# Two encoder layers on one core: memory keys at the head of layer 1, first loads reordered, more transposes by DMA

## The chip, the cores and the metric

One Trainium2 chip, one of its cores. The time is the device time of one execution in microseconds (us). The kernel before took 2009.22 us (median of three runs, 2007.9 to 2009.52). The core's engines each run their own program in order: PE (TensorE, the matmuls and the transposes through the identity), ACT (ScalarE), DVE (VectorE), POOL (GpSimd) and SP (SyncE, which here only issues loads). DMA queues belong to SP, ACT and POOL.

## The reference

A trunk of two layers (the depth is set to 2) over 256 tokens of width 2048, in float32, with 256 memory tokens:

```python
for l in range(DEPTH):                       # 2
    h = rms_norm(x, g_mix[l])
    if l % 2 == 0:                           # layer 0: spatial gating
        z = h @ w_in_a[0]                    # 2048 x 3584: u | v (1536 each), q_mem (512)
        tok_out = chunked_spatial_gating(...)   # u * (w_s @ rms_norm(v) + b_s), after a gelu
    else:                                    # layer 1: grouped-query attention, 12 heads on 4
        z = h @ w_in_b[0]                    # 2048 x 3072: q (1536), k, v (512 each), q_mem (512)
        tok_out = gqa_axial_attention(...)   # per-head rms norm, rotary, softmax
    mem_out = memory_attention(q_mem, mem, g_mem[l], w_mem_kv[l], g_mq[l], g_mk[l])
    x = x + concatenate([tok_out, mem_out]) @ w_out[l]
    x = x + swiglu(rms_norm(x, g_ffn[l]), w_gate_up[l], w_down[l])
```

`memory_attention` normalises the memory, multiplies it with `w_mem_kv` (keys: its first 512 columns, values: the next 512), normalises queries and keys per head, and does a softmax attention over 256 memory tokens with four heads.

## The kernel before, in words

**Products.** Each float32 operand is split into a high and a low part; `matmul3` (L181 to L183) issues high x high, low x high and high x low. `transpose4` (L185) turns four 128x128 blocks on PE (L187). `Linear` (L269) computes 256 tokens x 512 columns over K = 2048, that is 16 chunks of 128, in 96 matmuls of 128x512. Weights come as units of four K chunks: one load on SP's queue (L279), casts to the high part on ACT in pieces of two chunks (L265) and the low part on DVE (L266). Four raw tiles and three high and low tiles go round, so a cast waits until PE is done with the unit three before.

**Activations.** The residual stream lies in SBUF as `X[t][j]`: token tile t (0, 1) by a quarter j of the width (512 columns). For a linear its pieces are needed transposed and multiplied with the norm's gain, as high part (ACT, L225 or L237) and low part (DVE, L226 or L238). The norm's 1/rms itself is applied behind the product, so a linear may start ahead of it. A piece is turned either on PE (`norm_piece`, L209) or by `turned` (L189): ACT copies the words' halves apart (L194), issues a DMA transpose on its queue (L195), and later copies the halves back (L200), for which it waits until the transfer has landed. `add_residual` (L608) does that for one j, plus the squares of the norm (`square_sum`, L207, two per piece). In the feed-forward's last part of layer 0, `residual_turns` (L624) does it for layer 1's input: j=0,1 after the first pair of output columns, j=2,3 at the very end.

**Memory.** `prep` (L574) loads eight tiles of the transposed memory on POOL's queue (L577) and multiplies each with its gain three ticks later (`gained_pair`, L231: two products on ACT at L237 and two on DVE at L238 per tile). `keys` and `values` are one linear each over these tiles. In both layers they stand behind the memory queries' linear; in layer 1 that is behind all other linears of the mixer but the output's.

**The order.** `later(n, fn)` puts work n ticks ahead on a queue; a linear ticks twice in four K chunks. This sets the order in which instructions are recorded. A scheduler with its own model of times then lays down each engine's program; the engines run these strictly in order.

**The first linear.** In layer 0 it takes `x_t`, the transposed input, in eight loads, between them the weights in units of one, one and two chunks, and the eight loads of X (L135). Its outputs go through a Gelu (L727), whose scale is the norm, so all sixteen squares of X come before it. Meanwhile nine small matmuls warm PE up (L686).

**The feed-forward** (L776 on) uses a Strassen-like scheme in pairs of column blocks; no line of it is touched except `residual_turns`.

Of the kernel before, what the change touches and what calls it, by code (L numbers as in the profile page):

```python
# [17 lines left out]
P = 128  # L18
# [10 lines left out]
NB = 512  # L29
# [26 lines left out]
def encoder(ctx: ExitStack, tc: tile.TileContext, x, x_t, mem, mem_t, columns, w_in_a, g_v_a, spatial_t, w_in_b,  # L56
# [212 lines left out]
    class Linear:  # L269
# [3 lines left out]
            self.parts, self.w, self.n0, self.left, self.first, self.raw = parts, w, n0, nk, True, {}  # L273
            self.acc = [psa.tile([P, NB], F32, tag="acc", name=nm("acc")) for _ in range(NT)]

        def fetch(self, k0, n):
            raw = wp.tile([P, KC4, NB], F32, tag="raw", name=nm("raw"), bufs=RAW_TILES)
            src = self.w[k0 * P:(k0 + n) * P, self.n0:self.n0 + NB]
            nc.sync.dma_start(raw[:, :n], src.rearrange("(c p) n -> p c n", p=P))  # L279
            self.raw[k0] = raw  # L280

        def run(self, units):
            for k0, n in units:
                if k0 not in self.raw:
                    self.fetch(k0, n)
                raw = self.raw.pop(k0)
                parts = halves(raw[:, :n], n, KC2)
                for s in range(0, n, KC2):
                    m = min(KC2, n - s)
                    self.left -= m  # L290
                    for t in range(NT):
                        for c in range(m):
                            matmul3(self.acc[t], self.parts.get(k0 + s + c, t), parts[s + c],
                                    self.first and c == 0, self.left == 0 and c == m - 1)
                    self.first = False
                    tick()
            return self.acc
# [188 lines left out]
                nc.vector.tensor_tensor(lo[pr][:, :, ts], src, hi[pr][:, :, ts].bitcast(F32), ALU.subtract)  # L486
        return hi, lo

    def attend(qn, waits, keys, values, kv_of, kc0, parts):


        st = {}

        def head(p, h):
            return p[0][h // 2][:, h % 2, :], p[1][h // 2][:, h % 2, :]

        def queries():
            st["qT"] = heads_T(qn)

        def scores(pr):  # L500
            for h in (2 * pr, 2 * pr + 1):
# [13 lines left out]
                rcp = small(2)  # L515
                nc.vector.reciprocal(rcp, sm)
                for t in range(NT):
                    nc.vector.tensor_scalar(pe[:, t * S:(t + 1) * S], pe[:, t * S:(t + 1) * S], rcp[:, t:t + 1], None,
                                            ALU.mult)
                st["p", h] = pe  # L520

        def turn(pr):
            for h in (2 * pr, 2 * pr + 1):
                pn = st["p", h]
                pt = misc()
                for t in range(NT):
                    for kc in range(2):
                        nc.tensor.transpose(pt[:, kc * S + t * P:kc * S + (t + 1) * P],  # L528
                                            pn[:, t * S + kc * P:t * S + (kc + 1) * P], ident)
                st["t", h] = split(pt, [P, NB])  # L530

        def weigh(pr):
            V = values()
            po = misc()
            for hh in range(2):
                h = 2 * pr + hh
                kv = kv_of(h)
                phi, plo = st["t", h]
# [29 lines left out]
    class Memory:  # L568
# [5 lines left out]
        def prep(self, delay, apart):  # L574
            def load(i):
                m = big(shape=[P, 2, S])
                nc.gpsimd.dma_start(m, mem_t[:, 2 * i:2 * i + 2])  # L577
                later(3, lambda: gained_pair(m, i, gslice("mem", self.l), self.parts, big))
                if self.l == 0:
                    j, t = i // 2, i % 2  # L580
                    rows = big()
                    nc.gpsimd.dma_start(rows, mem[0, t * P:(t + 1) * P, j * NB:(j + 1) * NB])
                    later(3, lambda: squares(rows, j, t))

            def squares(rows, j, t):
                self.norm.add(rows, t, j)
                if (j, t) == (3, NT - 1):
                    self.norm.finish(self.r)

            for i in range(8):  # L590
                later(delay + apart * i, lambda i=i: load(i))

        def keys(self):
            acc = linear(self.parts, w_mem_kv[self.l], 0)
# [6 lines left out]
        def values(self):  # L601
            self.V = scaled(linear(self.parts, w_mem_kv[self.l], NB), self.r)

        def attend(self, acc, r, parts):
            attend(head_norm(acc, r, ghead[f"mq{self.l}"]), (4, 13, 17, 19), lambda: self.kT, lambda: self.V, lambda h: h,
                   TOK // P, parts)

    def add_residual(acc, j, norm, g, parts, dma):  # L608

# [12 lines left out]
            later(1 + t, lambda t=t: turn(t))  # L622

    def residual_turns(j, norm, g, parts):  # L624
        add_residual(None, j, norm, g, parts, j < 2)


    hT = Parts()
# [1 line left out]
    for l in range(DEPTH):  # L630
# [4 lines left out]
        if l == 0:  # L635
# [27 lines left out]
                nc.vector.tensor_tensor(v4(sb[t][c]), v4(sps), bcast4(bcol[:, 4 * c:4 * c + 4]), ALU.add)  # L663

            def turn_u(us, t, c):
                tp = misc()
                transpose4(us, tp)
                hi, lo = split(v4(tp), [P, 4, P])
                for i in range(4):
                    cat.put(4 * c + i, t, hi[:, i, :], lo[:, i, :])  # L670

            def load_turned(i, engine=nc.sync):
                turned_x[i] = big(shape=[P, 2, S])
# [13 lines left out]

            turned_x = {}
            lin = Linear(hT, w, TOK)
            load_turned(0, nc.scalar)  # L690
            nc.scalar.dma_start(cols, columns)
            nc.scalar.activation(junk[:, :8], mhalf, AF.Square)
            warm_up(9)
            lin.fetch(0, 1)
            lin.fetch(1, 1)
            load_turned(1)
            lin.fetch(2, 2)
            first_piece(0)
            lin.run([(0, 1)])
            load_turned(2)  # L700
            load_turned(3)
            lin.run([(1, 1)])
            first_piece(1)
            lin.run([(2, 2)])
            for i in range(2, 8):
                first_piece(i)
                if i % 2 == 0 and i < 6:
                    load_turned(i + 2)
                    load_turned(i + 3)
                lin.run([(2 * i, KC2)])  # L710
            for t in range(NT):
                for j in range(4):
                    load_x(t, j)
            load_tables(0)
            for j in range(4):
                first_squares(j)
            norm.finish()
            acc = lin.acc
            m.prep(1, 2)
            for i in range(3):  # L720
                later(10 + i, lambda i=i: load_spatial(i))
            for c in range(3):
                if c:
                    acc = linear(hT, w, TOK + c * NB)
                for t in range(NT):
                    v[t][c] = big()
                    nc.scalar.activation(v[t][c], acc[t], AF.Gelu, scale=norm.r[t])  # L727
                    square_sum(v[t][c], ssv[t][:, 2 * c:2 * c + 2])
            for t in range(NT):
                gate_rms(t)  # L730
                for c in range(3):
                    later(3 + 3 * t + c, lambda t=t, c=c: gate(t, c))
            m.attend(linear(hT, w, 2 * TOK), norm.r, cat)
            m.keys()
            m.values()
            for c in range(3):
# [6 lines left out]
        else:  # L743
            w = w_in_b[0]
            own = {}
            load_tables(1)
            m.prep(20, 2)
            acc = linear(hT, w, TOK)
            kn = head_norm(acc, norm.r, ghead["k"], True)

# [5 lines left out]
            for c in range(3):  # L756
                acc = linear(hT, w, c * NB)
                attend(head_norm(acc, norm.r, ghead["q"], True), (5, 6, 10, 13), lambda: own["k"], lambda: own["v"],
                       lambda h, c=c: (4 * c + h) // 3, 4 * c, cat)
            m.attend(linear(hT, w, TOK + 2 * MEMW), norm.r, cat)  # L760
            m.keys()
            m.values()

        hF = Parts()
# [130 lines left out]
```

## Time and profile before

| What | Value |
|---|---|
| time, median of 3 runs | 2009.22 us |
| the profiled execution's time | 2011.89 us |
| its span, first to last instruction | 2010.0 us |
| busy: PE, DVE, ACT, POOL | 1994.3, 1587.4, 1204.0, 60.3 us |
| mean granted PE clock | 0.998 |
| moved by DMA | 413.85 MB, 206 GB/s on average |
| first matmul of layer 1 | at 1007.5 us |

A row of the groups reads: line, engine, operation, written tile <- read tiles, shape, count, then busy us and mean ns of one, then the engine's idle time before them and what ended it. A row of the chain reads: start, length, what. Times are us from the span's start. In the names, `raw` is a loaded weight tile, `whi`/`wlo` its two parts, `h` and `a` activations, `m` a small PSUM tile, `acc` an accumulator, `x` the residual stream, `cols` the gains, `junk` the unused output of a square.

### The profile page before, as it was taken

The page shows a single profiled execution, that of the slowest core. Times are in us where ns is not written, and L with a number is a line of the kernel's source. Part 1 is how long each engine was busy: PE and PEld are TensorE (multiplying, and loading weights), DVE is VectorE, ACT ScalarE, POOL GpSimd, SP SyncE. Part 2 cuts the span into 40 slices and gives each one's busy share as a digit, 9 for nine tenths or more (in the row PEclk, how much of TensorE's full clock was granted, in tenths as well). Part 3 has the DMA queues.
Part 4 walks back from the last instruction along what each step waited for, and adds up shares of the span by engine and source line. Part 5 has one row for each costly group of instructions (what it writes and reads, how often), then busy time and mean ns, then how long its engine had stood idle before and what let it go on. Part 6 is the DMA issues. An engine that isn't in the chain of part 4 may idle for free.

```text
span 2010.0 us, 23977 instructions
## 1 busy us (share of the span) xinstructions
PE 1994.3 (99%) x8996; PEld 1652.5 (82%) x8996; DVE 1587.4 (79%) x1686; ACT 1204.0 (60%) x1450; POOL 60.3 (3%) x88
## 2 busy tenths in 40 slices
PE   8999999999999999999999999999999999999999
PEld 7888888888888888887888888888888888888787
DVE  5755558998988989886666876699988889888877
ACT  7755475666446664465765665856764467644662
POOL 2100001000000000000011000010000000000000
PEclk9999999999999999999999999999999999999999
DMA  9854675676666776657766434756766567665674
GB/s 354 288 177 159 194 214 182 206 218 212 220 209 189 213 217 223 208 187 230 224 220 199 163 122 154 217 188 198 229 214 219 189 199 232 214 214 188 199 209 147
DMA packets 266404, 413.85 MB, mean 206 GB/s; under 512 B 74640, under 2 KB 74896, under 8 KB 266288
## 3 DMA queue, kind: packets, MB, share of 16 engines
q1 hardware_dynamic: 199808, 387.62, 58.1%
q10 hardware_dynamic: 63792, 16.19, 4.7%
q0 software_dynamic: 2688, 8.52, 1.3%
q8 instruction: 70, 1.15, 0.2%
q14 instruction: 46, 0.38, 0.1%
HBM read 394.45 MB, written 2.10 MB: 197 GB/s over the span
## 4 chain that ended last, share of the span: by engine, by line
PE 93%; DMA 3%; DVE 2%; ACT 1%; issue 1%; ACTq 0%; SPq 0%; DVEq 0%
PE acc L183 27%; PE acc L182 27%; PE acc L181 27%; PE m L183 4%; PE m L181 4%; PE m L182 4%; DMA a<-a 2%; DVE wlo L266 1%; ACT whi L265 1%; PE m L187 1%; DMA a<-in_x_t 0%; DMA x<-in_x 0%; PE m L528 0%; PE m L661 0%; DMA raw<-in_w_in_a 0%
## 5 line engine op out<-in xcount | busy, mean ns | idle before, releaser
L266 DVE TENSOR_TENSOR wlo<-raw,whi 128x2048 fp32r<-128x2048 f32 (+2 forms) x465 | 841.2, 1824 | 280.4 <-ACT whi L265 267.7
L265 ACT CAST whi<-raw 128x2048 fp32r<-128x2048 f32 (+2 forms) x465 | 705.9, 1538 | 474.8 <-PE acc L182 375.1
L181 PE MATMUL acc<-whi,h 128*128 128x512 f32 x1440 | 561.9, 391 | 4.5 <-ACT whi L265 2.7
L182 PE MATMUL acc<-whi,h 128*128 128x512 f32 x1440 | 561.6, 390 | 0.0
L183 PE MATMUL acc<-wlo,h 128*128 128x512 f32 x1440 | 516.3, 391 | 0.8 <-DVE wlo L266 0.8
L181 PE MATMUL acc<-whi,a 128*128 128x512 f32 x1062 | 414.3, 391 | 1.2 <-DVE a L459 1.2
L182 PE MATMUL acc<-whi,a 128*128 128x512 f32 x1062 | 414.4, 390 | 0.0
L183 PE MATMUL acc<-wlo,a 128*128 128x512 f32 x1062 | 399.1, 390 | 0.2 <-DVE wlo L266 0.2
L181 PEld LDWEIGHTS acc<-whi,h 128*128 128x128 f32 x1440 | 270.6, 188 | 61.1 <-ACT whi L265 4.0
L183 PEld LDWEIGHTS acc<-wlo,h 128*128 128x128 f32 x1440 | 270.8, 188 | 58.6 <-DVE wlo L266 2.9
L182 PEld LDWEIGHTS acc<-whi,h 128*128 128x128 f32 x1440 | 270.9, 188 | 56.2 <-DVE h L238 0.4
L181 PEld LDWEIGHTS acc<-whi,a 128*128 128x128 f32 x1062 | 199.8, 188 | 43.2 <-DVE a L459 1.6
L183 PEld LDWEIGHTS acc<-wlo,a 128*128 128x128 f32 x1062 | 199.8, 188 | 41.7 <-DVE wlo L266 0.6
L182 PEld LDWEIGHTS acc<-whi,a 128*128 128x128 f32 x1062 | 199.7, 188 | 40.9
L265 ACT CAST whi<-T 128x1536 fp32r<-128x1536 f32 x82 | 121.4, 1480 | 103.4 <-PE acc L182 93.8
L266 DVE TENSOR_TENSOR wlo<-T,whi 128x1536 fp32r<-128x1536 f32 x82 | 143.6, 1751 | 11.0 <-ACT whi L265 11.0
L364 DVE TENSOR_TENSOR T<-raw 128x1024 f32<-128x1024 f32 x82 | 100.0, 1220 | 21.5 <-DMA raw<-in_w_gate_up 20.7
L181 PE MATMUL m<-whi,a 128*128 128x512 f32 x264 | 102.8, 390 | 0.2 <-ACT whi L265 0.2
L183 PE MATMUL m<-wlo,a 128*128 128x512 f32 x264 | 102.8, 389 | 0.1
L182 PE MATMUL m<-whi,a 128*128 128x512 f32 x264 | 102.7, 389 | 0.0
L200 ACT COPY sg<-a 128x1024 uint16<-128x1024 uint16 x44 | 51.5, 1169 | 47.0 <-DMA a<-a 46.8
L441 DVE TENSOR_TENSOR e<-acc,e 128x512 f32<-128x512 f32 x88 | 58.1, 684 | 2.5 <-PE acc L183 2.5
(120 smaller groups left out, 1432.9 us busy)
## 6 DMA issues: line engine op xcount, KB each, us to landing
raw<-in_w_gate_up SPq DMA_DIRECT2D x352, 512.0 KB, 4.4
raw<-in_w_down SPq DMA_DIRECT2D x176, 512.0 KB, 4.9
raw<-in_w_out SPq DMA_DIRECT2D x32, 1024.0 KB, 5.3
raw<-in_w_in_a SPq DMA_DIRECT2D x24, 1024.0 KB, 5.3
raw<-in_w_in_b SPq DMA_DIRECT2D x24, 1024.0 KB, 5.2
raw<-in_w_mem_kv SPq DMA_DIRECT2D x16, 1024.0 KB, 5.1
a<-in_mem_t POOLq DMA_DIRECT2D x16, 256.0 KB, 5.3
raw<-in_w_in_a SPq DMA_DIRECT2D x7, 512.0 KB, 7.2
```

The source lines that it names most:

```text
L181: nc.tensor.matmul(out, lhsT=a[0], rhs=b[0], start=start, stop=False)
L182: nc.tensor.matmul(out, lhsT=a[1], rhs=b[0], start=False, stop=False)
L183: nc.tensor.matmul(out, lhsT=a[0], rhs=b[1], start=False, stop=stop)
L187: nc.tensor.transpose(dst[:, c * P:(c + 1) * P], src[:, c * P:(c + 1) * P], ident)
L200: nc.scalar.copy(halves, back.rearrange("p (h n) -> p n h", h=2))
L265: nc.scalar.copy(hi[:, cut], raw[:, cut])
L266: nc.vector.tensor_tensor(lo[:, cut], raw[:, cut], hi[:, cut].bitcast(F32), ALU.subtract)
L364: nc.vector.tensor_tensor(T[:, :2], raw[:, 1:4:2], w01, ALU.add)
L441: nc.vector.tensor_tensor(o[t][n], self.bank[name], o[t][n], op)
```

## The change

Four things, which the diff below shows:

1. *The start.* The gains (`cols`) are loaded first on ACT's queue and all `x_t` on SP's. The first linear's weights come in units of four chunks, cut into loads of 256 or 512 KB; X is loaded behind all of them. The squares, the norm's end and the first Gelu are put off by ticks (1 to 4, 5 and 6). The warm-up has sixteen matmuls. The memory's loads are called with `prep(3, 2)`.
2. *Layer 0's turns.* The six tiles of u and the memory attention's four probability tiles are turned by `turned` and no longer on PE (24 and 16 transposes), the latter with other waits (4, 13, 17, 21).
3. *Between the layers.* The residual pieces j=2,3 are turned by DMA too (16 transposes of PE fewer).
4. *Layer 1.* `prep(-4, 1)` and the memory keys' linear stand ahead of the layer's other linears; `prep(0, 1)` loads and multiplies the memory again for the values, whose linear is last, behind the memory queries and their attention (waits 4, 5, 9, 11).

`prep` now counts its ticks from one point, and work whose tick has passed is recorded at once (`soon`).

```diff
@@ class Linear
-        def fetch(self, k0, n):
-            raw = wp.tile([P, KC4, NB], F32, tag="raw", name=nm("raw"), bufs=RAW_TILES)
-            src = self.w[k0 * P:(k0 + n) * P, self.n0:self.n0 + NB]
-            nc.sync.dma_start(raw[:, :n], src.rearrange("(c p) n -> p c n", p=P))
-            self.raw[k0] = raw
+        def fetch(self, k0, n, cuts=None):
+            if k0 not in self.raw:
+                self.raw[k0] = wp.tile([P, KC4, NB], F32, tag="raw", name=nm("raw"), bufs=RAW_TILES)
+            for c, m in cuts or [(0, n)]:
+                src = self.w[(k0 + c) * P:(k0 + c + m) * P, self.n0:self.n0 + NB]
+                nc.sync.dma_start(self.raw[k0][:, c:c + m], src.rearrange("(c p) n -> p c n", p=P))
@@ def attend(..., dma=False), def turn(pr)
+                if dma:
+                    def halves_of(whole, h=h):
+                        hi, lo = split(whole.rearrange("p (t k) n -> p k t n", t=NT), [P, 2, NT, P])
+                        st["t", h] = [a.rearrange("p k t n -> p (k t n)") for a in (hi, lo)]
+
+                    turned(pn, 2, halves_of, True)
+                    continue
@@ class Memory, def prep(self, delay, apart)
-                later(3, lambda: gained_pair(m, i, gslice("mem", self.l), self.parts, big))
+                soon(delay + apart * i + 3, lambda: gained_pair(m, i, gslice("mem", self.l), self.parts, big))
...
+            now = clock[0]
+
+            def soon(at, fn):
+                if now + at <= clock[0]:
+                    fn()
+                else:
+                    later(now + at - clock[0], fn)
+
             for i in range(8):
-                later(delay + apart * i, lambda i=i: load(i))
+                soon(delay + apart * i, lambda i=i: load(i))
@@ def residual_turns(j, norm, g, parts)
-        add_residual(None, j, norm, g, parts, j < 2)
+        add_residual(None, j, norm, g, parts, True)
@@ layer 0, def turn_u(us, t, c)
-                tp = misc()
-                transpose4(us, tp)
-                hi, lo = split(v4(tp), [P, 4, P])
-                for i in range(4):
-                    cat.put(4 * c + i, t, hi[:, i, :], lo[:, i, :])
+                def parts(whole):
+                    hi, lo = split(whole, [P, 4, P])
+                    for i in range(4):
+                        cat.put(4 * c + i, t, hi[:, i, :], lo[:, i, :])
+
+                turned(us, 2, parts, True)
@@ layer 0, the start (after)
+            nc.scalar.dma_start(cols, columns)
+            load_turned(0)
+            lin.fetch(0, KC4, [(0, 1), (1, 1)])
+            warm_up(16)
...
+            lin.run([(0, KC4)], 1)
...
+            lin.run([(8, KC4)])
             for t in range(NT):
                 for j in range(4):
                     load_x(t, j)
             load_tables(0)
+            for i in (6, 7):
+                first_piece(i)
+            lin.run([(12, KC4)])
             for j in range(4):
-                first_squares(j)
-            norm.finish()
+                later(1 + j, lambda j=j: first_squares(j))
+            later(5, norm.finish)
             acc = lin.acc
-            m.prep(1, 2)
+            m.prep(3, 2)
...
+            later(6, lambda: gated(0, acc))
+            for c in (1, 2):
+                gated(c, linear(hT, w, TOK + c * NB))
...
-            m.attend(linear(hT, w, 2 * TOK), norm.r, cat)
+            m.attend(linear(hT, w, 2 * TOK), norm.r, cat, (4, 13, 17, 21), True)
@@ layer 1
-            m.prep(20, 2)
+            m.prep(-4, 1)
+            m.keys()
             acc = linear(hT, w, TOK)
             kn = head_norm(acc, norm.r, ghead["k"], True)
...
-            m.attend(linear(hT, w, TOK + 2 * MEMW), norm.r, cat)
-            m.keys()
+            m.prep(0, 1)
+            m.attend(linear(hT, w, TOK + 2 * MEMW), norm.r, cat, (4, 5, 9, 11), False)
             m.values()
```

How the engines' programs change at the places the prediction speaks of. ACT at the start, where the first linear ends (`x_0`, `x_1` are X; L727 and, in the changed kernel, L750 are the Gelu; each cast is of weights). Before:

```order
L265 CAST whi_315<-raw_313 128x1024 [waits DMAHW1_49,DVE_49,PE_49]
L207 ACTIVATE junk,s_1_91<-x_1_85 128x256 [waits DMAHW3_49,Activation_49]
L207 ACTIVATE junk,s_1_91<-x_1_85 128x256 [waits Activation_49]
L207 ACTIVATE junk,s_2_92<-x_1_87 128x256 [waits DMAHW7_49,Activation_49]
L207 ACTIVATE junk,s_2_92<-x_1_87 128x256 [waits Activation_49]
L265 CAST whi_383<-raw_381 128x1024 [waits DMAHW2_49,DVE_49,PE_49]
L265 CAST whi_383<-raw_381 128x1024
L727 ACT_TABLE_LOAD [waits PE_49]
L727 ACTIVATE a_371<-acc_103,s_64_363 128x512 [waits Pool_49]
```

and now, from the last cast of the first linear's weights to the first cast of the second's (between the rows with `x_0` and `x_1` stand eleven more squares):

```order
L265 CAST whi_307<-raw_238 128x1024 [waits DMAHW1_49]
L207 ACTIVATE junk,s_1_91<-x_0_84 128x256 [waits DMAHW2_49]
L207 ACTIVATE junk,s_1_91<-x_0_84 128x256 [waits Activation_49]
L207 ACTIVATE junk,s_2_92<-x_0_86 128x256 [waits DMAHW6_49,Activation_49]
...
L207 ACTIVATE junk,s_2_92<-x_1_87 128x256 [waits DMAHW1_49,Activation_49]
L207 ACTIVATE junk,s_2_92<-x_1_87 128x256 [waits Activation_49]
L750 ACT_TABLE_LOAD [waits PE_49]
L750 ACTIVATE a_471<-acc_103,s_62_447 128x512 [waits Pool_49]
L265 CAST whi_341<-raw_339 128x1024 [waits DMAHW2_49,DVE_49]
```

Before, three of the first linear's casts stood between the squares, and the second linear's first cast (`whi_383`) stood ahead of the table load. Now all sixteen squares stand in one run, and that cast (`whi_341`) stands behind the Gelu.

ACT between the layers, from the squares of the last residual pieces on. Before (`m` are PE's transposes, `whi_7745` and `whi_7777` weights of layer 1's first linear):

```order
L265 CAST whi_7745<-raw_7743 128x1024
L207 ACTIVATE junk,s_415_2564<-x_1_87 128x256 [waits DVE_49,Activation_49]
L225 ACTIVATE h_7624<-m_7619,cols 128x128 [waits PE_49]
...
L207 ACTIVATE junk,s_415_2564<-x_1_87 128x256 [waits Activation_49]
L225 ACTIVATE h_7624<-m_7619,cols 128x128 [waits DVE_49]
L225 ACTIVATE h_7641<-m_7636,cols 128x128 [waits PE_49]
...
L265 CAST whi_7777<-raw_7775 128x1024 [waits DMAHW5_49,PE_49]
```

and now (each L237 row is the first of a memory tile's two products: `a_7593` is K chunks 0 and 1 of the keys' linear, `a_7601` 2 and 3, `a_7647` 4 and 5, `a_7691` 6 and 7; the fourth copy back and four more tiles follow):

```order
L207 ACTIVATE junk,s_410_2558<-x_1_87 128x256 [waits Activation_49]
L237 ACTIVATE a_7593<-a_7591,cols 128x256 [waits DMASW6_49]
L237 ACTIVATE a_7601<-a_7599,cols 128x256 [waits DMASW7_49]
...
L194 COPY a_7635<-x_1_85 128x1024
L195 DMA_TRANSPOSE a_7636<-a_7635 128x8x128 [waits Activation_49]
L194 COPY a_7641<-x_1_85 128x1024
L200 COPY a_7635<-a_7636 128x1024 [waits DMAHW3_49]
L195 DMA_TRANSPOSE a_7642<-a_7641 128x8x128 [waits Activation_49]
L237 ACTIVATE a_7647<-a_7607,cols 128x256 [waits DMASW0_49]
...
L200 COPY a_7667<-a_7668 128x1024 [waits DMAHW5_49]
L195 DMA_TRANSPOSE a_7674<-a_7673 128x8x128 [waits Activation_49]
L237 ACTIVATE a_7691<-a_7609,cols 128x256 [waits DMASW1_49]
```

Before, no product at L237 stood near the boundary; the memory came later. Now all eight tiles' products stand behind the last squares, six of them between or behind the four turns. On PE the keys' 96 matmuls are the first of layer 1, and none of another linear stands between them.

POOL between the layers, now (`in_mem_t` is the memory, L165 and L168 are the norm's scale and pow):

```order
L585 DMA a_7591<-in_mem_t 128x512 [waits DMAHW5_49,DMASW6_49]
L165 TENSOR_SCALAR s_1241_7681<-s_1240_7679 128x1 [waits DVE_49]
L165 TENSOR_SCALAR s_1244_7687<-s_1243_7685 128x1 [waits DVE_49]
L160 TENSOR_SCALAR a_7584<-a_7584 128x128 [waits DMASW2_49]
L168 TENSOR_TENSOR s_1242_7683<-s_1241_7681,mhalf 128x1 [waits Pool_49]
L168 TENSOR_TENSOR s_1245_7689<-s_1244_7687,mhalf 128x1 [waits Pool_49]
L160 TENSOR_SCALAR a_7584<-a_7584 128x128 [waits DMASW4_49]
L585 DMA a_7599<-in_mem_t 128x512 [waits DMASW7_49]
```

One memory tile is loaded ahead of the norm's end, the others behind it; before, all eight stood further down. At the start POOL now issues four memory loads right behind the first two gains, ahead of the norm; before, the first memory load stood behind it.

More of the change, by code (lines that the diff above doesn't have):

```diff
@@ L274, in __init__, with run @@
             self.acc = [psa.tile([P, NB], F32, tag="acc", name=nm("acc")) for _ in range(NT)]
[L276 to L282 removed]
+        def fetch(self, k0, n, cuts=None):
[4 more added lines that the diff above has]
+                nc.sync.dma_start(self.raw[k0][:, c:c + m], src.rearrange("(c p) n -> p c n", p=P))
+        def run(self, units, step=KC2):
             for k0, n in units:
@@ L286, in run @@
                 raw = self.raw.pop(k0)
-                parts = halves(raw[:, :n], n, KC2)
+                parts = halves(raw[:, :n], n, step)
                 for s in range(0, n, KC2):
@@ L487, in heads_T, with attend @@
         return hi, lo
-    def attend(qn, waits, keys, values, kv_of, kc0, parts):
+    def attend(qn, waits, keys, values, kv_of, kc0, parts, dma=False):
         st = {}
@@ L582, in load @@
                     nc.gpsimd.dma_start(rows, mem[0, t * P:(t + 1) * P, j * NB:(j + 1) * NB])
-                    later(3, lambda: squares(rows, j, t))
+                    soon(delay + apart * i + 3, lambda: squares(rows, j, t))
             def squares(rows, j, t):
@@ L602, in values, with attend @@
             self.V = scaled(linear(self.parts, w_mem_kv[self.l], NB), self.r)
-        def attend(self, acc, r, parts):
-            attend(head_norm(acc, r, ghead[f"mq{self.l}"]), (4, 13, 17, 19), lambda: self.kT, lambda: self.V, lambda h: h,
-                   TOK // P, parts)
+        def attend(self, acc, r, parts, waits, dma):
+            attend(head_norm(acc, r, ghead[f"mq{self.l}"]), waits, lambda: self.kT, lambda: self.V, lambda h: h, TOK // P,
+                   parts, dma)
     def add_residual(acc, j, norm, g, parts, dma):
@@ L689, in encoder @@
             lin = Linear(hT, w, TOK)
-            load_turned(0, nc.scalar)
             nc.scalar.dma_start(cols, columns)
+            load_turned(0)
+            lin.fetch(0, KC4, [(0, 1), (1, 1)])
             nc.scalar.activation(junk[:, :8], mhalf, AF.Square)
-            warm_up(9)
-            lin.fetch(0, 1)
-            lin.fetch(1, 1)
+            warm_up(16)
             load_turned(1)
-            lin.fetch(2, 2)
+            lin.fetch(0, KC4, [(2, 2)])
+            for i in (2, 3):
+                load_turned(i)
             first_piece(0)
[L699 to L702, printed above, removed]
+            lin.fetch(4, KC4, [(0, 2), (2, 2)])
             first_piece(1)
-            lin.run([(2, 2)])
-            for i in range(2, 8):
-                first_piece(i)
[L707 to L710, printed above, removed]
+            for i in (4, 5):
+                load_turned(i)
+            lin.run([(0, KC4)], 1)
+            lin.fetch(8, KC4, [(0, 2), (2, 2)])
+            for i in (6, 7):
+                load_turned(i)
+            for i in (2, 3):
+                first_piece(i)
+            lin.run([(4, KC4)])
+            lin.fetch(12, KC4, [(0, 2), (2, 2)])
+            for i in (4, 5):
+                first_piece(i)
+            lin.run([(8, KC4)])
             for t in range(NT):
@@ L714, in encoder, with gated @@
             load_tables(0)
+            for i in (6, 7):
+                first_piece(i)
+            lin.run([(12, KC4)])
             for j in range(4):
-                first_squares(j)
-            norm.finish()
+                later(1 + j, lambda j=j: first_squares(j))
+            later(5, norm.finish)
             acc = lin.acc
-            m.prep(1, 2)
+            m.prep(3, 2)
             for i in range(3):
                 later(10 + i, lambda i=i: load_spatial(i))
-            for c in range(3):
-                if c:
-                    acc = linear(hT, w, TOK + c * NB)
+            def gated(c, acc):
                 for t in range(NT):
```

## The prediction

> **What bounds the kernel now.** I read the page first (busy shares, the chain that ended last), then the chain row by row at the places the change touches, then the windows around them.
>
> ```profile
> span 2010.0 us, 23977 instructions
> PE 1994.3 (99%) x8996; PEld 1652.5 (82%) x8996; DVE 1587.4 (79%) x1686; ACT 1204.0 (60%) x1450; POOL 60.3 (3%) x88
> PE 93%; DMA 3%; DVE 2%; ACT 1%; issue 1%; ACTq 0%; SPq 0%; DVEq 0%
> ```
>
> The chain is TensorE for 93%. So a change can gain only by giving PE less to do, or by closing the few places where it stands idle; and it can lose wherever PE's next operand comes late. What PE does per instruction, and that it does not pause between layer 0 and layer 1, the chain shows there (start, length, what):
>
> ```profile
> 1007.42 0.23 PE acc L183
> 1007.65 0.23 PE acc L181
> ...
> 1014.04 0.87 PE m L187 x8
> ```
>
> A 128x512 matmul takes 0.227 us of PE's time (a linear's 96 are 21.8 us), eight transposes take 0.87 us. Layer 1's first matmul follows layer 0's last at 1007.5 with no gap. Windows of the stretches concerned (window, length, busy of PE, PEld, DVE, ACT, POOL, granted clock, DMA share, GB/s):
>
> ```profile
> 0.00:34.00 34.00, 28.76 (x115) 22.50 (x116) 17.72 (x29) 26.39 (x62) 4.92 (x17) 0.95 0.98 342
> 1007.50:1030.00 22.50, 22.50 (x109) 18.71 (x108) 15.08 (x27) 14.88 (x34) 3.10 (x6) 1.00 0.58 191
> 1153.00:1163.00 10.00, 8.02 (x34) 6.20 (x33) 8.88 (x25) 7.46 (x26) 2.52 (x2) 0.83 0.46 161
> 1187.00:1192.00 5.00, 3.73 (x25) 3.06 (x24) 3.81 (x13) 5.00 (x17) 0.00 (x0) 1.00 0.00 1
> ```
>
> The boundary costs nothing today. The start is bound by the loads (DMA share 0.98). In layer 1's attention PE idles 1.98 + 1.27 us, and the clock of 0.83 over 10 us means some 3.4 us at half speed, 1.7 us lost: 5.0 us in all.
>
> **Transposes taken from PE.** u: 6 tiles of 4 = 24; layer 0's memory probabilities 16; residual pieces j=2,3 16. 56 x 0.87/8 = **-6.1 us**, if what they become is covered. A DMA turn is a copy at L194, an issue at L195 and a copy back at L200, all on ScalarE, which runs in order and stands at L200 until the transfer lands.
>
> ```profile
> L195 ACTq DMA_TRANSPOSE a<-a x4: 1248/1248/1249, 972.8 to 986.2; - x4
> DMA to landing us min/median/max: 3.0/4.0/5.2
> ...
> L195 ACTq DMA_TRANSPOSE a<-a x4: 1248/1249/1299, 364.6 to 408.3; - x4
> DMA to landing us min/median/max: 3.9/5.8/9.2
> ```
>
> These are L195's four turns shortly before the boundary and four amid layer 0's feed-forward: issue 1.25 us, landing 3.0 to 5.2 and up to 9.2. ScalarE's waits (total, times, longest):
>
> ```profile
> ACT whi L265 <- PE acc L182: 468.9, 183, 4.6
> ACT sg L200 <- DMA a<-a: 46.8, 19, 5.8
> ```
>
> In layer 0 the cover is ScalarE's own slack: its weight casts wait for a free buffer, that is for PE, 468.9 us in all, so they run ahead. A turn takes up to 5.8 us of wait there; only the last u tile, whose consumer follows at once, may show. Cost 0 to 1.2 us (1.04 + 1.25 + 3.0 + 1.17 beside the ticks it is given), taken as **+0.5**. Without the cover it is 2.5 us (46.8/19) for each of ten turns: a rival.
>
> [...]
>
> **The boundary.** Now the order of the programs decides. Before, the first linear of layer 1 used the residual pieces j=0,1, long ready; j=2,3 had 48 matmuls (10.9 us) of cover. Now the first linear is the memory keys. Their operands are eight products at L237 on ScalarE, and in its program these stand behind and between the last norm squares and the four DMA turns of j=2,3, as the order rows above show. Durations there, by lines and by groups (times in ns, or busy us and mean ns):
>
> ```profile
> L207 ACT ACTIVATE junk<-x x8: 402/418/419, 1005.0 to 1011.5; 128x256 f32<-128x256 f32 x8
> L577 POOL DMA_DIRECT2D a<-in_mem_t x3: 546/563/614, 1037.7 to 1038.9; - x3
> DMA to landing us min/median/max: 3.1/3.8/3.8
> L168 POOL TENSOR_TENSOR s<-s,mhalf 128x1 f32<-128x1 f32 (+1 forms) x3 | 2.7, 917 | 0.2
> L265 ACT CAST whi<-raw 128x1024 fp32r<-128x1024 f32 x199 | 199.5, 1048 | 107.9 <-PE acc L182 88.1 <-DMA raw<-in_w_in_a 11.1 <-issue 5.5
> L200 ACT COPY a<-a 128x1024 uint16<-128x1024 uint16 x16 | 18.7, 1168 | 9.3 <-DMA a<-a 9.2
> L194 ACT COPY a<-x 128x1024 uint16<-128x1024 uint16 x16 | 16.6, 1040 | 16.5 <-DVE x L621 16.1 <-DVE x L441 0.4
> L237 ACT ACTIVATE a<-a,cols 128x256 fp32r<-128x256 f32 x32 | 14.4, 503 | 0.0
> L225 ACT ACTIVATE h<-a,cols 128x128 fp32r<-128x128 f32 x64 | 20.4, 391 | 0.0
> ```
>
> Let E be the end of layer 0's last matmul. The squares end at about E+4.3 (today 1011.8), so the first product is there at E+4.8. The second memory tile is loaded by GpSimd only behind the norm's pow steps (0.9 us each): issue E+6.5, landing 3.1 to 3.8 later, products done E+10.6. Then ScalarE still has, ahead of the last product: four turns x (1.04 + 1.25 + 1.17) = 13.8, four times four h pieces x 0.39 = 6.3, two tiles' casts x 2.1 = 4.2, six tiles' products x 1.0 = 6.0: together 30.3 us, with no landing counted. Walking the rows with a landing of 3.0 adds 0.6 us of waits, with 5.2 some 4.6. So the last tile's first product comes at E+41.2 to 45.2, its 12 matmuls take 2.7, and the keys end at E+43.9 to 47.9 where 21.8 would do. Lost: 22.1 to 26.1 us; and up to 2.7 more if the clock is at half for the last 12 matmuls, as it fell to 0.83 after today's stall. I take **+25** (22 to 29). VectorE's half of each product follows ScalarE's within its own 0.5 us. Behind it nothing is late: weights and DMA catch up meanwhile.
>
> [...]
>
> **The start.** Today, from the timeline (start, length), ScalarE and GpSimd:
>
> ```profile
> 31.67 1.98 ACT L265 CAST whi<-raw 128x1024 fp32r<-128x1024 f32 x2
> 33.66 1.28 ACT L727 ACT_TABLE_LOAD   x1
> 34.96 1.27 ACT L727 ACTIVATE a<-acc,s 128x512 f32<-128x512 f32 x2
> ...
> 7.75 0.30 POOL L160 TENSOR_SCALAR a<-a 128x128 f32<-128x128 f32 x1 [5.03 <-DMA a<-in_g_mq]
> 32.84 0.61 POOL L577 DMA_DIRECT2D a<-in_mem_t  x1
> ```
>
> The matmuls between 33 and 34.2 us, the loads of X, and the pace of the squares in the chain:
>
> ```profile
> L181 PE MATMUL acc<-whi,h x2: 389/389/389, 33.1 to 33.8; 128*128 128x512 f32 x2
> ...
> L135 SPq DMA_DIRECT2D x<-in_x x8: 328/328/328, 10.6 to 18.1; - x8
> DMA to landing us min/median/max: 6.4/7.1/7.4
> ...
> 22.60 0.52 ACT junk L207 x2
> ...
> 23.68 0.52 ACT junk L207 x2
> ```
>
> The second linear's first matmul starts at 33.8, right after the first linear; its weights' cast (31.67 to 33.65) stands before the Gelu's table load. After, X is loaded behind all weights, all sixteen squares stand behind the last weights, and table load and Gelu, which need them, stand ahead of that cast. Of 32 pieces of 256 KB (8.4 MB at 342 GB/s, 0.77 us each) the fifth of X is the 29th: it lands at about 25.6 (4.0 + 28 x 0.77). Today's eighth lands at 24.5 to 25.5 (18.1 + 6.4 to 7.4). The four memory loads that GpSimd now issues at once, not at 32.84, share that rate: up to +3.1. From 25.6 to 28.7 on: 14 squares at 0.54 (two in 23.68 - 22.60) = 7.6, the norm's sum and pow some 1.5 with the table load 1.28 beside them, one Gelu 0.64, the cast's first half 1.05: second linear at 36.4 to 39.5 and not 33.8. The first linear ends earlier (29 to 32), but that only lengthens the gap, and a gap that long costs up to 1.7 us at half clock. +2.6 to +7.4; I take **+5**. The warm-up's seven extra matmuls lie in PE's idle time before its data.
>
> **Layer 1's attention.** Later transposes after the softmax (waits 4, 5, 9, 11), the values' linear last as cover, but the second copy of the memory preparation adds 16 products each on ScalarE and VectorE (8 x 1.0 us) and eight loads in the same stretch. Gain 0 to 5.0, the two stalls' whole price; I take **-3**.
>
> **Sum:** -6.1 + 0.5 + 25 + 5 - 3 = +21.4 against the profiled execution, which took 2011.89 us (span 2010.0 and 1.89 around it): 2033.3. The median of the runs is 2009.22, 2.67 lower; so the median after is **2031 us**, +1.1%. By the ends of the terms: -6.1 + 0 + 22 + 2.6 - 5 = +13.5 and -6.1 + 1.2 + 28.8 + 7.4 - 0 = +31.3.
>
> **Rivals.** (1) *The start gains.* If X lands early enough for the squares to end before the first linear does, the second follows at once at about 29.8: -4 in place of +5, 2022 us. For it: weights and x_t come first, in 256 KB pieces. Against: 7.6 us of squares behind the fifth piece of X. 0.12. (2) *The boundary is covered, and it is faster.* If the eight memory products run during layer 0's last work, the keys' 21.8 us hide all four turns: -6.1 + 0.5 + 0 + 5 - 3 = -3.6, 2005.6 us. It decides as soon as the first keys matmul comes within 1 us of E. For it: ScalarE is busy 60%. Against: its order, in which two products wait for the last squares and six for the turns. 0.05. (3) *Landings at the boundary are long,* since weight loads run beside them: 9.2 us (the longest above) and not 3 to 5 puts some 3.5 us onto each of four waits, +14: 2045 us. Against: weight loads stop when their buffers are full, within some microseconds of PE's stall. 0.05. (4) *Layer 0's turns are not covered:* each of ten holds the casts up by its wait and PE with them, 10 x 2.5 us, 2056 us. For it: casts and turns share ScalarE's one order. Against: 468.9 us of casts waiting for PE. 0.04. [...] (5) The change does not do what it says, and all waits stay as they are: 2009. The orders differ at every place named. 0.02.
>
> **Numbers.** Forecast 0.72 and (1) give slower; so do (3) and (4): 0.93. Faster by over 0.2% (4 us, about what a measurement of this kernel can tell from none) 0.05; within it 0.02. Range 2016 to 2042: from rival (1) with the low ends of the boundary and of layer 1 (2022 - 3 - 2) and a run's spread below it, to the high sum (2009.2 + 31.3 = 2040.5) and as much above; left out are the faster case, no change and the two dear rivals.
>
> **What would show it.** Right: PE's idle between 1000 and 1055 some 22 to 29 us, in four or five gaps that wait for L237; an L237 behind each L200; a first gap of 5 us, then one to E+10; the second linear's first matmul at 36 to 40, waiting for the cast at L265 behind the Gelu; no wait for L175 after L200 in layer 0 above 1.2 us. Wrong: keys that start at E, an end of the keys by E+30, or a span below 2015.

## The result, and the profile after

The changed kernel takes 2035.51 us (median of 4 runs, 2034.07 to 2035.9), the kernel before 2009.37 us (4 runs). The ratio is 1.0129, 95% interval 1.0111 to 1.0146: 26 us slower. The forecast was 2031 us, range 2016 to 2042.

The page of the changed kernel, first lines:

```profile
span 2034.1 us, 23972 instructions
PE 1997.2 (98%) x8954; PEld 1652.8 (81%) x8954; DVE 1593.4 (78%) x1703; ACT 1239.3 (61%) x1495; POOL 62.9 (3%) x96
PE 91%; DMA 4%; ACT 2%; DVE 2%; issue 1%; SPq 0%; POOL 0%; ACTq 0%; DVEq 0%; POOLq 0%
```

PE is still the chain, but it holds 91% and not 93% of it: DMA and ScalarE have moved in. PE's busy time has hardly changed, although 56 transposes are gone, because a matmul at half clock counts as busy for longer (0.43 us from start to start and not 0.227), and the longer warm-up counts too (6.2 us of PE and not 3.6). Shares do not show the loss; PE's waits do (what waited for what: total, times, longest):

```profile
PE acc L181 <- ACT a L237: 18.3, 5, 6.7
PE acc L181 <- ACT whi L265: 8.8, 3, 5.3
```

Before, the longest of PE's waits behind the start was 1.4 us. Now four of the waits for a memory product (L237) lie between the layers, 17.9 us together, and one of 5.3 us for a weight cast lies at the start. The windows of the start, the boundary and the attention (window, length, busy of PE, PEld, DVE, ACT, POOL, granted clock, DMA share, GB/s):

```profile
0.00:34.00 34.00, 29.75 (x128) 24.65 (x128) 16.52 (x26) 22.35 (x50) 4.42 (x14) 0.95 0.96 335
34.00:44.00 10.00, 4.66 (x13) 3.40 (x12) 3.81 (x7) 9.81 (x24) 6.84 (x14) 0.66 1.03 372
1012.00:1059.00 47.00, 29.09 (x99) 22.00 (x98) 21.85 (x43) 31.18 (x64) 7.24 (x13) 0.82 0.55 161
1204.00:1212.00 8.00, 6.32 (x43) 5.17 (x42) 8.00 (x13) 7.88 (x26) 0.23 (x1) 1.00 0.55 153
```

The chain of waits between the layers shows step by step why PE stood (start, length, what; E, the end of layer 0's last matmul, is 1012.2):

```profile
1012.15 0.24 PE acc L183
...
1013.64 0.94 ACT whi L265
...
1016.10 0.52 ACT junk L207 x2
1016.64 0.17 DVE s L256
...
1017.76 1.14 POOL s L168 x2
...
1019.35 3.23 DMA a<-in_mem_t
1022.61 0.91 ACT a L237 x2
1023.52 0.94 ACT a L194
1024.48 4.72 DMA a<-a
1029.23 1.17 ACT a L200
...
1031.44 1.17 ACT h L225 x4
1032.61 1.88 ACT whi L265 x2
1034.49 0.95 ACT a L194
1035.47 5.88 DMA a<-a
1041.37 1.17 ACT a L200
...
1042.67 0.52 ACT a L237
1043.23 1.22 PE acc L181 x2
```

It is the chain of the forecast: squares, the norm's pow on GpSimd, only then the second memory tile's load, then ScalarE's turns with their landings, then the fourth tile's product at E+30.5. From there PE runs through (60 matmuls in 15.7 us, 13.6 without the half clock of the first ones) and ends the keys at E+46.7.

To compare kernels I use **PE's loss**: over all pairs of successive matmuls, the time between their starts beyond a dense pace (0.227 us for 512 columns, 0.118 for 256, 0.109 for 128; the medians in the trace of before are 0.227, 0.120 and 0.109), summed over a stretch. It holds waits and half clock alike. The warm-up's small matmuls count as dense work: 32 records with the new start, 18 with the old one (before, e3, e4, e8). So the start column is 14 x 0.109 = 1.5 us too low for the new start when the two are compared.

| Kernel | start (to 48 us) | rest of layer 0 | boundary | attention | after 1300 us | ratio to before |
|---|---|---|---|---|---|---|
| before | 8.7 | 3.3 | 0.1 | 6.9 | 2.4 | 1 |
| changed | 15.1 | 4.4 | 24.8 | 4.5 | 1.1 | 1.0129 (1.0111 to 1.0146) |
| e1: layer 1's order as before | 15.9 | 5.4 | 8.2 | 5.3 | 2.8 | 1.0039 (1.0025 to 1.0054) |
| e2: j=2,3 turned on PE | 15.6 | 2.5 | 9.3 | 4.4 | 5.7 | 1.0053 (1.0037 to 1.0068) |
| e3: start as before | 8.9 | 5.4 | 25.8 | 4.5 | 3.3 | 1.0082 (1.0067 to 1.0097) |
| e4: before + layer 0's turns | 9.2 | 11.8 | 0.1 | 6.8 | 3.5 | 0.9987 (0.9976 to 0.9999) |
| e6: memory loads late at the start | 7.6 | 5.5 | 25.9 | 4.4 | 1.1 | 1.0094 (1.0076 to 1.0113) |
| e8: keys second | 9.0 | 4.7 | 0.7 | 4.4 | 7.9 | 0.9983 (0.9971 to 0.9996) |
| e9: keys second, new start | 4.9 | 4.2 | 0.7 | 4.4 | 3.2 | 0.9956 (0.9942 to 0.9970) |
| e10: pieces of j=2,3 made twice | 16.1 | 3.2 | 26.1 | 4.5 | 4.6 | 1.0124 (1.0106 to 1.0143) |
| e11: e9 with DMA turns of j=2,3 | 4.8 | 2.9 | 14.9 | 4.4 | 4.9 | 1.0019 (1.0006 to 1.0031) |
| e12: e9 with layer 0's turns on PE | 4.9 | 3.9 | 0.6 | 4.4 | 2.3 | 0.9964 (0.9950 to 0.9978) |
| e13: turns behind the products | 17.0 | 2.9 | 9.8 | 4.4 | 7.0 | 1.0054 (1.0033 to 1.0075) |

Changed against before: +7.9 at the start (6.4 and the warm-up's 1.5), +1.1 in layer 0, +24.7 at the boundary, -2.4 in the attention, -1.3 behind, -6.1 for 56 transposes: +23.9, where the profiled executions have 24.0 (2035.9 against 2011.89). The start shows directly, too: from the 111th matmul of 512 columns to the 331st, each starts 7.9 us later than before.

The experiments ran beside the kernel before at a median of 2015 to 2016 us (2010 to 2022), not 2009, so they are compared by their ratios and by PE's loss, and the microseconds in the expectations are to be read against 2009.

### The profile page after: what moved, and what is told of

Same layout as the page of the kernel before. It is cut to its first block, busy times and chain, and to the rows that moved or that the text cites. A ratio compares the mean times of both kernels' runs of the same rounds, so it can differ in the third digit from the quotient of the medians.

```text
span 2034.1 us, 23972 instructions
## 1 busy us (share of the span) xinstructions
PE 1997.2 (98%) x8954; PEld 1652.8 (81%) x8954; DVE 1593.4 (78%) x1703; ACT 1239.3 (61%) x1495; POOL 62.9 (3%) x96
## 4 chain that ended last, share of the span: by engine, by line
PE 91%; DMA 4%; ACT 2%; DVE 2%; issue 1%; SPq 0%; POOL 0%; ACTq 0%; DVEq 0%; POOLq 0%
PE acc L183 26%; PE acc L182 26%; PE acc L181 26%; PE m L181 4%; PE m L183 4%; PE m L182 4%; DMA a<-a 2%; DMA a<-in_x_t 1%; DVE wlo L266 1%; ACT whi L265 1%; PE m L187 0%; ACT junk L207 0%; DMA x<-in_x 0%; PE m L677 0%; ACT a L194 0%
## 5 line engine op out<-in xcount | busy, mean ns | idle before, releaser
L181 PE MATMUL acc<-whi,a 128*128 128x512 f32 x1062 | 414.5, 393 | 18.8 <-ACT a L237 18.3
L365 DVE TENSOR_TENSOR T<-raw 128x1024 f32<-128x1024 f32 x82 | 100.0, 1220 | 21.4 <-DMA raw<-in_w_gate_up 19.5
```

The source lines that it names most:

```text
L181: nc.tensor.matmul(out, lhsT=a[0], rhs=b[0], start=start, stop=False)
L365: nc.vector.tensor_tensor(T[:, :2], raw[:, 1:4:2], w01, ALU.add)
```

## The experiments

Theory A is the one of the forecast: ScalarE's in-order program (squares, turns, products) sets PE's wait at the boundary. Its rivals there: the keys' place alone costs, or the turns alone.

**e1, layer 1's order undone.**

```diff
-            m.prep(-4, 1)
-            m.keys()
+            m.prep(20, 2)
...
-            m.prep(0, 1)
-            m.attend(linear(hT, w, TOK + 2 * MEMW), norm.r, cat, (4, 5, 9, 11), False)
+            m.attend(linear(hT, w, TOK + 2 * MEMW), norm.r, cat, (4, 13, 17, 19), False)
+            m.keys()
             m.values()
```

> The changed kernel with the order of layer 1 as before (keys and values behind the memory queries, memory prepared once, old waits); the four DMA turns of j=2,3 stay. Theory A (ScalarE's one in-order chain of squares, turns and products sets PE's waits): the turns still hold up the first linear, which now needs j=2 after 48 matmuls; walking ScalarE's rows, the third turn's pieces are there at about E+27, so PE waits some 13 us and not 25, and layer 1's attention loses about 3 again: 2026 us. Rival B (the keys' place alone costs the boundary): the loss of 25 goes and 3 come back, 2013 us. Rival C (the turns' landing alone costs): nothing changes at the boundary, 2038 us.

Ratio 1.0039, 18 us below the change; 8.2 us lost at the boundary. The direction is A's, the size is not: 8 and not 13. So the turns alone still cost, without any memory product near, and the rival that the keys' place alone costs is out.

**e2, the four turns on PE again.**

```diff
-        add_residual(None, j, norm, g, parts, True)
+        add_residual(None, j, norm, g, parts, j < 2)
```

> The changed kernel with j=2,3 turned on PE as before (16 transposes back); keys stay first. Theory A: ScalarE does the squares and the sixteen pieces first, about 10 us, then the eight memory products; PE starts the keys at about E+10 and is fed from there on: 10 us lost and not 25, the transposes lie in the gap: 2020 to 2022 us. Rival B (the keys' place alone): 25 stay, 2036 us. Rival C (the turns alone): the loss goes whole, 2012 us.

Ratio 1.0053, 15 us below the change; 9.3 us lost at the boundary, 10 expected. One wait is left there:

```profile
PE acc L181 <- ACT a L237: 6.6, 1, 6.6
```

It is the first tile's product, behind all sixteen pieces of j=2,3, ten of them in one run. So the keys' place alone costs too. 8.2 and 9.3 add up to 17.5, less than 24.8: together they cost 7.3 us more than one by one.

**e13, the same work in another order.** The four turns start six ticks later, so that all eight products stand ahead of them on ScalarE; squares, transfers and everything else stay.

```diff
-                turned(X[t][j], 2, lambda a: gained(a.rearrange("p c n -> p (c n)"), t, j, g, parts, kept))
+                later(0 if acc or j < 2 else 6, lambda: turned(X[t][j], 2, lambda a: gained(a.rearrange("p c n -> p (c n)"), t, j, g, parts, kept)))
```

> The changed kernel, but the four DMA turns of j=2,3 start six ticks later (their squares stay): on ScalarE all eight memory products now stand ahead of all four turns, and nothing is taken away. Theory A (what stands ahead of a product on ScalarE sets PE's wait; the fourth tile decides, since PE needs 13.6 us for the rest): the first keys matmul at E+4.8, the second tile at E+10.5 as before, then one tile per us: 10 to 11 us lost by the keys; k's linear then waits 0 to 6 us for the late turns: 10 to 17 at the boundary in place of 24.8, a ratio of 1.006 to 1.009. Rival (the four turns cost what they cost, wherever they stand, by ScalarE's and the DMA's work): 24 to 26 again, ratio 1.0125.

9.8 us at the boundary in place of 24.8, ratio 1.0054, and only two waits (PE's waits from 1000 to 1060 us):

```profile
PE acc L181 <- ACT a L237: 5.8, 2, 4.7
```

Its windows of the boundary, columns as above:

```profile
1012.50:1030.00 17.50, 11.69 (x41) 8.85 (x40) 9.15 (x15) 11.10 (x26) 7.23 (x13) 0.80 0.70 237
1030.00:1045.00 15.00, 15.00 (x68) 12.43 (x67) 7.98 (x13) 11.55 (x19) 0.00 (x0) 1.00 0.79 207
```

4.7 us wait for the squares and 1.1 for the second tile's load; the granted clock was 0.80 in the first window and 1.00 in the second. From 1030 on PE is full, while the same four turns run beside it. This settles it: 15 of the 25 us came from what stood ahead on ScalarE, not from the amount of work. k's linear, which I gave up to 6 us of waiting for the late turns, did not wait.

**e10, more work in the chain.** ScalarE makes each high piece of j=2,3 twice.

```diff
+            for _ in range(times):
-            nc.scalar.activation(hi[:, c, :], v4(tp)[:, c, :], AF.Copy, scale=gc)
+                nc.scalar.activation(hi[:, c, :], v4(tp)[:, c, :], AF.Copy, scale=gc)
```

> The changed kernel, but ScalarE makes the sixteen pieces of j=2,3 twice (the second time over the first, so nothing else changes). Twelve of the repeats stand ahead of the last memory product on ScalarE, 0.3 us each. Theory A (ScalarE's busy time between the end of layer 0 and the last product sets the gap): PE's loss at the boundary grows by 2.3 to 3.5 us, from 24.8 to 27 to 28.3. Rival (the landings of the turns and the memory loads set it, ScalarE has slack between): it stays within 0.5 us of 24.8.

26.1 us, +1.3, between the two, and kernels with an untouched boundary (e3, e6) have 25.8 and 25.9: inconclusive. The products, first and last start (this kernel, then the changed one):

```profile
L238 ACT ACTIVATE a<-a,cols x16: 491/493/508, 1016.3 to 1054.1; 128x256 fp32r<-128x256 f32 x16
```

```profile
L237 ACT ACTIVATE a<-a,cols x16: 492/499/509, 1016.5 to 1051.6; 128x256 fp32r<-128x256 f32 x16
```

The last product did come 2.5 us later, as expected, but PE no longer waited for it: the fourth is the one that decides, and only four repeats stood ahead of that, inside a wait for a landing. The expectation took the wrong product.

**e3, the start undone,** its lines exactly as before.

> The changed kernel with the start as before (loads, warm-up, squares, Gelu and the memory's first loads). If the new start costs what the profile shows (second linear 5.9 us later, then 2.2 us at half clock): 8 us less, 2027 to 2028 us. Rival: the start's delay is made up later in layer 0, 2033 to 2035 us.

Ratio 1.0082, 9.5 us below the change; PE's loss at the start falls from 15.1 to 8.9, that is by 7.7 with the warm-up's 1.5. Nothing was made up later.

**e6, the start's memory loads later.**

```diff
-            m.prep(3, 2)
+            m.prep(9, 2)
```

> The changed kernel with the memory's first loads recorded six ticks later in layer 0, so that GpSimd issues them behind the norm; with it ScalarE's first cast of the second linear moves ahead of the last three squares and the Gelu. Theory A (at the start the memory loads take the bandwidth that the first linear waits for, and the squares hold the second one up): the first linear ends at about 30 and not 34.2 us, X lands 2.7 us earlier, the second linear starts at 35 to 36 and not 39.7 us: 4 us less than the changed kernel, a ratio to before of 1.011. Rival (the memory loads do not matter, the squares' order alone does): the second linear starts at 38 or later, ratio 1.0125 or more.

Ratio 1.0094, 7 us below the change; loss 7.6 at the start in place of 15.1, which with the warm-up's 1.5 is 0.4 us more than before's 8.7. The first linear ended at 31.2 and not 34.2 us, the second began at 33.7 and not 39.7. The first linear's loads (from issue to landing, and who waited), of the changed kernel and of e6:

```profile
  ACT whi L265: 5.2, 6
DMA to landing us min/median/max: 3.7/9.0/10.8
```

```profile
  ACT whi L265: 3.3, 5
DMA to landing us min/median/max: 3.6/8.0/8.5
```

So the four memory loads on GpSimd's queue did two things: they took bandwidth from the first weights (a 3.1 us wait of PE at 10.3 us and a clock of 0.50 from 13.05 to 16.47 us behind it, where e6 has 0.9 us and a clock of 1.00 to 34 us), and moved X back. Since the ticks also moved the scheduler's cast ahead of the Gelu, the run does not tell the two parts of the 7.5 us apart.

**e4, layer 0's turns alone,** on the kernel before (`turn_u` and `turn` as in the change, with its waits for layer 0).

> The kernel before with layer 0's turns alone changed (u and the memory's probabilities by DMA, waits 4, 13, 17, 21). If the turns are covered but for the small waits seen after the change (1.3 us around 185 to 190 us): 40 transposes, 4.35, less 1.3: 3 us less, 2006 us. Rival (the turns' waits on ScalarE reach PE): 2009 us or more.

Ratio 0.9987 (0.9976 to 0.9999), -2.6 us, as expected. The 11.8 us in its row for layer 0 are mostly waits for weights' loads spread over the feed-forward, 344 to 928 us, where nothing was changed.

**e8 and e9, a version to beat both.** e8: before's start, layer 0's DMA turns, PE turns between the layers, the change's attention, and the keys as the second linear of layer 1. e9 adds a start of its own.

```diff
-            m.prep(-4, 1)
-            m.keys()
+            m.prep(1, 1)
             acc = linear(hT, w, TOK)
...
             later(7, turn_k)
+            m.keys()
```

```diff
-                    load_x(t, j)
+                    later(4, lambda t=t, j=j: load_x(t, j))
...
-                later(1 + j, lambda j=j: first_squares(j))
+                later(2 + j, lambda j=j: first_squares(j))
...
-            m.prep(3, 2)
+            m.prep(10, 2)
```

> The start as before, layer 0's turns by DMA, j=2,3 turned on PE, the memory keys as the second linear of layer 1 (behind k), the memory prepared from tick 1 on, and the attention as in the change (second preparation, values last). Theory A: k's linear covers the products and no gap is left at the boundary (under 0.5 us); the attention's stalls cost 4.4 and not 6.9 us of PE's time; 40 transposes, 4.35, less some 1.5 in layer 0: 5 us less than before, ratio 0.9973. Rival: the products on ScalarE get ahead of the pieces of j=2,3 and the casts, a gap of 3 to 8 us at the boundary: ratio 0.999 to 1.002.

> The same as the one with the keys second, with another start: the changed kernel's units and order of the first loads, but X behind the second linear's first weights, the squares behind that linear's first cast, and the memory loads behind the norm. Theory A: the first linear ends at 29 to 30 us and the second follows at once: 4 us less than with the start of before, ratio 0.9953. Rival: the loads between 30 and 57 us cannot keep up and PE waits for weights then: no better than 0.9973.

e8 has no gap at the boundary (0.7 us in all) and 4.4 us in the attention, and 0.9983 (0.9971 to 0.9996): the sign as expected, 3.4 us and not 5. Its profiled execution lost 7.9 us after 1300 us (before: 2.4), in code that is the same. e9 comes to 0.9956 (0.9942 to 0.9970), 9 us faster than before and 35 faster than the change. Its start:

```profile
0.00:34.00 34.00, 32.46 (x145) 27.22 (x146) 18.72 (x28) 24.22 (x53) 2.31 (x10) 1.00 0.98 341
34.00:44.00 10.00, 9.35 (x41) 7.06 (x40) 5.06 (x7) 9.91 (x21) 4.24 (x10) 1.00 1.02 362
```

PE is busy from the first weights on at full clock, and the second linear's first cast ran at 25.6 us, ahead of squares and Gelu. X, the squares and the memory loads all moved, so the run does not tell what each is worth.

**e11 and e12, single parts of the change on e9.** e11 turns j=2,3 by DMA, e12 turns u and the probabilities on PE.

> The fast version (keys second, new start) with j=2,3 turned by DMA: part 3 of the change alone, beside otherwise equal code. Theory A: k's linear has 48 matmuls, 10.9 us, before it needs j=2, the four turns take ScalarE some 20 us: PE loses 8 us at the boundary as with the keys late, 16 transposes less give back 1.7: 6 us more than the fast version, ratio 0.9988. Rival (the turns only cost together with the keys' products): within 1 us of the fast version or faster, ratio 0.995.

> The fast version with layer 0's turns on PE as before: part 2 of the change alone, beside otherwise equal code. Theory: 40 transposes back, 4.35, less the waits of the turns in layer 0, 1 to 1.5: 3 us more than the fast version, ratio 0.997. Rival (the DMA turns gain nothing in sum): ratio 0.9956 or less.

e11: 1.0019, 12.7 us slower than e9, twice what I expected; 14.9 us at the boundary. The first of its turns landed late (the group of the transposes, then who waited for it and from issue to landing):

```profile
L195 ACTq DMA_TRANSPOSE a<-a x4: 1249/1249/1250, 1003.8 to 1021.4; - x4
  ACT a L200: 8.1, 1
DMA to landing us min/median/max: 3.1/4.5/10.9
```

The window of that landing, columns as above:

```profile
1003.80:1014.60 10.80, 7.67 (x34) 6.01 (x32) 0.26 (x1) 1.82 (x5) 3.72 (x8) 1.00 0.92 207
```

Over the 10.9 us of that landing the DMA queues were busy at 0.92, with weights and with memory tiles of GpSimd's queue; that they made it long is likely, but no run shows it. e12: 0.9964 against 0.9956; the intervals overlap, so what layer 0's turns gain in this version (1.6 us by the medians, 3.1 by the two profiles) is not settled.

## Why the prediction was right

**The boundary (+25 forecast, +24.7 of PE's loss)** was the case by its own mechanism, and its milestones came as walked through: the first product let PE go at E+4.85 (4.8 forecast), the second tile's load issued at E+7.15 (6.5) and landed at E+10.4 (9.6 to 10.3), the fourth product at E+30.5, the last at E+39.5 (41.2 to 45.2), the keys' end at E+46.7 (43.9 to 47.9). Three details were off. I let the last product decide; it was the fourth, as PE needs 13.6 us from there on. I gave half clock at most 2.7 us; it took 6.0, and the four gaps 18.8 (4.85, 1.9, 5.0 and 7.05) where I had 22.1 to 26.1. These two errors offset each other, so it is in part luck that 24.7 lies so near to 25. And I added every issue of a turn, 1.25 us, to ScalarE's time. Three of the four ran beside a copy back, as here (start, length):

```profile
1029.23 1.16 ACT L200 COPY a<-a 128x1024 uint16<-128x1024 uint16 x1 [2.41 <-DMA a<-a]
1029.23 1.25 ACTq L195 DMA_TRANSPOSE a<-a  x1
```

So the last product came early, although ScalarE waited 4.8 us for landings. The landings lay with 4.72 and 5.88 us inside the chain, near my upper value of 5.2.

**The start (+5, bounds 2.6 to 7.4; +7.9)** had the right mechanism and was mis-sized, 0.5 us beyond its bound. The fifth piece of X landed at 29.1 (25.6 to 28.7), the second linear began at 39.7 (36.4 to 39.5), 5.9 us later than before, and half clock (0.50 from 36.95 to 43.77 us) took 2.0 us and not at most 1.7. "The first linear ends earlier (29 to 32)" did not come either: it ended at 34.2. I had charged the memory loads to X alone, and they held up the first linear's own weights by 3.1 us too. That delay cost nothing more here, as the second linear was waiting for squares, Gelu and cast.

**Transposes (-6.1)** are right by count; e4's ratio, -2.6 us for 40 of them with their waits, fits it. **Layer 0's turns (+0.5):** +1.1 in the table, three waits between 185 and 190 us; in other runs the stretch to 240 us cost 0.3 to 2.2 us. So the bound of 1.2 held in this execution and would not in each. The rival in which every turn costs 2.5 us is out by e4.

**Attention (-3, bounds 0 to -5; -2.4)** came for the most part by luck. Of before's 6.9 us, 1.6 are half clock (0.50 from 1157.9 to 1161.3). In e1 the attention is as before, with the same four pauses of PE (1.57, 0.74, 0.86 and 0.74 us), but no half clock followed, and 5.3 us were lost; the last section has the windows of both. Against that the change gains 0.8 us; e8, with nothing else near, has the same 4.4.

The sum, +21.4, fell 4.7 short of 26.1: 2.6 in the terms above and behind 1300 us, and 2.1 because the profiled execution of before lay 2.5 us above its median (2011.89 and 2009.37), that of after only 0.4. Of the rivals, "landings at the boundary are long" did not come in the change, but e11 shows one: 10.9 us. "The boundary is covered" fell with the first keys matmul at E+4.85, "the start gains" with the second linear at 39.7.

## What to carry to other kernels

A transpose by DMA was cheap where its three steps on the issuing engine ran ahead of need (e4: 40 transposes moved, -2.6 us), and dear where the next operand of the bottleneck stood behind them in the same engine's program (24.8 us at the boundary, 9.8 in e13 with the same work behind the operands): look for what stands ahead of the first operand, not for how busy the engine is. The first linear of a stage should be one whose operands are long ready, and new preparations belong under its cover (e8: 0.7 us at the boundary). Where a program sets loads loose early, count whose bandwidth they take, on every queue (the first linear's weights took up to 10.8 us to land, in e6 up to 8.5).

## What the runs showed of the hardware

After three of the four gaps at the boundary of the changed kernel the matmuls started every 0.43 us and not every 0.227 us for some time. The granted clock, by stretch of the changed kernel:

```profile
1017.10:1022.90 5.80, 4.32 (x12) 3.15 (x12) 0.85 (x2) 0.60 (x2) 5.52 (x11) 0.75 0.87 282
1022.90:1030.90 8.00, 3.10 (x12) 2.10 (x12) 0.88 (x2) 4.12 (x6) 0.30 (x1) 0.96 0.75 200
1030.90:1043.20 12.30, 5.49 (x12) 3.80 (x12) 5.52 (x12) 9.51 (x18) 0.00 (x0) 0.64 0.49 131
1043.20:1058.90 15.70, 15.67 (x61) 12.80 (x62) 11.16 (x22) 12.04 (x27) 0.00 (x0) 0.87 0.31 81
```

In its trace the clock was 0.50 from 1016.6 to 1020.0, from 1030.2 to 1037.0 and from 1040.5 to 1047.3, that is for 3.4, 6.8 and 6.8 us, and 1.00 between. Behind the second gap (PE's last start before it at 1021.0, the next at 1023.2) it stayed at 1.00. In sum the half clock was a quarter of the boundary's loss (6.0 of 24.8 us).

Half clock did not follow each pause, and in the three cases below it did not follow the longest. The two pauses of 1.57 and 0.74 us in the attention were followed by half clock in the kernel before (first fence: two windows behind one another, each as long as that half clock, 3.41 us; columns as above), and not in e1 (second fence). In e6 a pause of 2.5 us at the start was not followed by it either (third fence). The clock is the last figure but two: 0.50 in the second row of before, 1.00 in all others. No run varied the pauses alone, so what decides is not shown.

```profile
1154.48:1157.89 3.41, 1.57 (x8) 1.23 (x9) 3.31 (x9) 3.41 (x11) 0.00 (x0) 1.00 0.13 46
1157.89:1161.31 3.42, 3.42 (x10) 2.64 (x9) 3.42 (x9) 2.01 (x9) 1.62 (x2) 0.50 0.26 49
```

```profile
1165.09:1168.50 3.41, 2.06 (x14) 1.58 (x12) 2.37 (x8) 3.34 (x12) 0.00 (x0) 1.00 0.78 293
1168.50:1171.92 3.42, 2.78 (x13) 2.20 (x14) 3.42 (x8) 3.32 (x14) 0.00 (x0) 1.00 0.00 0
```

```profile
29.15:32.57 3.42, 2.23 (x10) 1.50 (x8) 0.00 (x0) 3.23 (x14) 0.00 (x0) 1.00 1.05 387
32.57:35.98 3.41, 2.20 (x8) 1.53 (x9) 2.44 (x3) 3.39 (x7) 0.76 (x2) 1.00 1.05 387
```

The landing of a residual piece's DMA transpose ranged from 3.0 us (before) to 10.9 us (e11); the longest came beside DMA queues that were 0.92 busy. No run varied their load alone.
